# Expert weights moved in 2 MB transfers of neighbouring matrix rows, with token columns and activations regrouped to match

## The chip, the core and the metric

The kernel runs on one core of a Trainium2 chip. The metric is the device time of one execution in microseconds (us), from the start of the program to its end; smaller is better. TensorE (PE in the profile) multiplies matrices, VectorE (DVE), ScalarE (ACT) and GpSimd (POOL) work on elements, and SyncE (SP) issues most of the transfers (DMAs) from the memory of the chip into the core's own. That memory has 128 partitions, and TensorE sums over partitions.

## The reference

A first block of two layers (feed-forward, token mixing, feed-forward) and a second block of one layer (attention, then a mixture of experts) on 256 tokens of 1024 numbers, all in float32. The change touches the last stage:

```python
def moe_ffn(h, w_router, b_router, w_gate_up, b_gate_up, w_down, b_down):
    logits = (h @ w_router).astype(jnp.float32) + b_router.astype(jnp.float32)
    top_val, top_idx = lax.top_k(logits, TOP_K)
    gates = jax.nn.softmax(top_val, axis=-1)
...
    def expert_block(args):
        xe, e = args
        gu = xe @ w_gate_up[e] + b_gate_up[e]
        g = jnp.minimum(gu[:, :D_FF_2], SWIGLU_LIMIT)
        u = jnp.clip(gu[:, D_FF_2:], -SWIGLU_LIMIT, SWIGLU_LIMIT)
        act = (u + 1.0) * (g * jax.nn.sigmoid(SWIGLU_ALPHA * g))
        return act @ w_down[e] + b_down[e]
...
    return jax.ops.segment_sum(y, tok_sorted, num_segments=n)
```

`TOP_K` is 4. An expert's weights are 1024 by 2048 numbers or 8 MB (`w_gate_up`) and 1024 by 1024 or 4 MB (`w_down`); the 32 experts have 384 MB, of the 638 MB that the whole program moves.

## The kernel before

The program runs through its stages once: the first block until about 1130 us, attention until about 1315, routing, and the experts from 1340 to the end. A scheduler puts each engine's instructions into a fixed order ahead of time; buffers come from pools, and a transfer into a buffer waits until the last reader of what was in it is done.

In the first block and attention (the dense part), `piece` (L145) and `natural_parts` (L361) load 1 MB of weights at a time into one of four `raw` buffers. `split` makes two float32r parts of each half: the upper on ScalarE (L177, `wh`, or `dh` for the rows of a feed-forward's second matrix), the rest on VectorE (L178). The last of these four operations frees the buffer.

For the experts, `moe_order` lists the weights in the order of use, 1 MB at a time: of `w_gate_up` eight pieces of 128 rows (a partition receives one row, 8 KB), of `w_down` four pieces of 256 rows (a partition receives two rows that lie 128 rows apart, 4 KB each). `moe_slots` names nineteen 1 MB places, used round and round: two of `rawE`, two halves of `xp`, six slots that attention had, four `raw`, four `raw2`, one `raw3`. `prefetch` issues the next transfer (L1159). Some are issued during attention and routing as places come free, the others as the experts use theirs.

An expert takes 64 places for tokens. For four experts at a time, `tokens` (L1188) selects their tokens of `h2` with matmuls against a 0/1 matrix; its stationary operand is 128 neighbouring columns of `h2`. `gate_up` multiplies (L1209) and adds the bias (L1213). A matmul here has 64 rows of output, and two of them, for the two halves of the columns, stand in different halves of the array. `down` for the expert before transposes the activations (L1227, 128 neighbouring columns each), multiplies (L1235), adds the bias (L1238), scales (L1240, VectorE), turns the gates (L1243, L1245), and adds the result to the tokens (L1249). `leave` (L1261 to L1264) copies the sums and sends them out. `overflow` repeats it for experts with over 64 tokens.

Of the kernel before, what the change touches and what calls it, by code (L numbers as in the profile page):

```python
# [16 lines left out]
P = 128  # L17
# [20 lines left out]
class Kernel:  # L38
    def __init__(self, ctx, tc, a, out):
# [4 lines left out]
        self.raw = pool("raw", 4)  # L44
# [8 lines left out]
        self.uid = 0  # L53
# [13 lines left out]
    # ---------------------------------------------------------------- constants  # L67
# [87 lines left out]
    def conv_block(self, w, h, l):  # L155
        """w = x @ weights, transposed."""
# [7 lines left out]
    def up_block_t(self, w, ab, h, l, t):  # L164
        """As up_block, for 128 tokens."""
# [5 lines left out]
    def split(self, v, low=None, pools=None):  # L171
        """v [P, k, f], 1024 numbers on a partition, as two float32r parts whose sum is v."""
# [16 lines left out]
    # ---------------------------------------------------------------- layer norm  # L189
# [9 lines left out]
    def rstd_wide(self, pool, var, eps, scale):  # L199
        """As rstd: by exponential and logarithm, then a step of Newton's."""  # L200
# [11 lines left out]
    def to_T(self, src, t, ks=range(KD), psum=None, halves=None):  # L212
        """Columns of src, 128 at a time, transposed into self.xT, or into halves, as two float32r parts."""
# [15 lines left out]
    def residual(self, acc, t, scale):  # L229
        """Adds the scaled residual to sums that matmuls have started."""  # L230
# [4 lines left out]
    def add_norm(self, pool, t, acc, eps, g, b, y):  # L235
        """xn[t] = layer norm of acc."""
# [22 lines left out]
    def up_ahead(self, w1, w3, small=False, low=None):  # L259
        """The first pieces, and their parts, one after another."""  # L260
# [92 lines left out]
    # ---------------------------------------------------------------- token mixing  # L353
    def natural_parts(self, srcs, n, q, low=None):
        """The parts of 512 rows of the columns that srcs name."""
        r = self.raw.tile([P, 2048], F32, tag="raw", name=self.n("raw"))
# [9 lines left out]
    def natural(self, srcs, n, parts=None):  # L366
        """[tokens, n] of x @ w for the columns that srcs name, as [P, 2, 512] of PSUM; with parts the first tokens first."""
# [1299 lines left out]
```

## Time and profile before

| | |
|---|---|
| three runs | 2287.51, 2284.88, 2289.31 us; median 2287.51 |
| span of the profiled execution (first to last instruction) | 2285.8 us |
| median less span | 1.7 us |
| TensorE busy | 2177.6 us, 95% of the span |
| first block, attention, routing | about 1340 us |
| experts | about 946 us |
| moved | 637.68 MB, 237193 packets |

The profile gives no time of its own for the profiled execution beyond the span. The time in which an engine is busy is an average over stages; the stages differ, so the rows further down are taken stage by stage. In the trace a float32 matmul leaves two records, so "x8" of L1235 are four matmuls. The trace leaves out no stage, but a few of TensorE's records can be missing.

### The profile page before, as it was taken

To read this page: it belongs to the slowest core of one execution; us is meant where nothing else is said; L and a number is where in the kernel's file an instruction comes from. 1 tells how busy PE (TensorE), PEld (TensorE's weight loads), DVE (VectorE), ACT (ScalarE), POOL (GpSimd) and SP (SyncE) were. 2 spreads that over 40 slices of the span, in tenths; PEclk is the share of its full clock that TensorE was granted. 3 is DMA by queue.
4 is the path that set the end of the run, shared out by engine and by line. 5 is a ranking of instruction groups with operands and counts; after the bars stand their busy time and mean duration, and the time that the engine had idled before them with its cause. 6 is when DMAs were issued, how large, how long until landed. Compare 5 with 4: busy or idle time off the path is not lost. (4 is left out here: it accounts for less than half of the span.)

```text
span 2285.8 us, 28097 instructions
## 1 busy us (share of the span) xinstructions
PE 2177.6 (95%) x11342; PEld 1366.5 (60%) x11343; DVE 1057.9 (46%) x1656; ACT 753.9 (33%) x1110; POOL 191.9 (8%) x216
## 2 busy tenths in 40 slices
PE   7999999999899999999989789999999999999998
PEld 6888877888788887788867553333333333333332
DVE  5866875966776687686676721111111111111111
ACT  4554842555355484255547410000000000000000
POOL 1001222001100122200020300000000000000000
PEclk8999998999999999899999779999999999999999
DMA  9855432956775443275654479999999999999997
GB/s 271 298 184 156 151 119 74 330 187 214 246 256 184 153 150 119 76 248 191 206 190 132 175 299 418 416 417 417 417 416 417 417 418 417 417 417 416 417 417 295
DMA packets 237193, 637.68 MB, mean 279 GB/s; under 512 B 27201, under 2 KB 134689, under 8 KB 204289
## 3 DMA queue, kind: packets, MB, share of 16 engines
q1 hardware_dynamic: 219664, 622.96, 72.0%
q0 software_dynamic: 4048, 11.28, 1.6%
q10 hardware_dynamic: 13344, 1.57, 0.5%
q8 instruction: 91, 1.49, 0.3%
q14 instruction: 46, 0.37, 0.0%
HBM read 633.91 MB, written 1.86 MB: 278 GB/s over the span
## 5 line engine op out<-in xcount | busy, mean ns | idle before, releaser
L178 DVE TENSOR_TENSOR wl<-raw,wh 128x1024 fp32r<-128x1024 f32 x332 | 407.9, 1234 | 190.5 <-ACT wh L177 189.0
L177 ACT ACTIVATE wh<-raw 128x1024 fp32r<-128x1024 f32 (+1 forms) x350 | 366.5, 1051 | 367.6 <-PE w L152 142.8
L1209 PE MATMUL w<-rawm,XT 128*64 128x512 f32 x2048 | 479.5, 597 | 3.0 <-ACT wh L1245 2.1
L152 PE MATMUL w<-xT,wh 128*128 128x512 f32 x1344 | 476.5, 396 | 5.1 <-DVE ab L288 5.1
L153 PE MATMUL w<-xT,wl 128*128 128x256 f32 x1344 | 378.8, 282 | 0.0
L1209 PEld LDWEIGHTS w<-rawm,XT 128*64 128x64 f32 x2048 | 145.5, 137 | 302.0 <-issue 289.2
L1216 DVE TENSOR_SCALAR wl<-w 128x512 f32<-128x512 f32 x32 | 22.1, 692 | 594.3 <-PE w L1213 594.3
L152 PEld LDWEIGHTS w<-xT,wh 128*128 128x128 f32 x1344 | 254.0, 189 | 65.5 <-DVE ab L288 5.8
L153 PEld LDWEIGHTS w<-xT,wl 128*128 128x128 f32 x1344 | 253.4, 189 | 1.6
L1235 PE MATMUL w<-rawm,wh 128*64 128x512 f32 x1024 | 237.3, 600 | 5.7 <-ACT wh L1229 3.7
L300 PE MATMUL m<-wh,gT 128*128 128x512 f32 x592 | 190.9, 393 | 0.0
L1229 ACT ACTIVATE wh<-w 128x512 f32<-128x512 f32 x32 | 19.1, 597 | 449.6 <-PE w L1227 443.0
L1235 PEld LDWEIGHTS w<-rawm,wh 128*64 128x64 f32 x1024 | 67.0, 136 | 145.3 <-issue 130.7
L300 PEld LDWEIGHTS m<-wh,gT 128*128 128x128 f32 x592 | 111.2, 188 | 26.8 <-issue 1.7
L1240 DVE TENSOR_TENSOR wl<-w,wl 128x512 f32<-128x512 f32 x32 | 22.1, 692 | 211.6 <-PE w L1238 211.6
L300 PE MATMUL m<-wl,gT 128*128 128x512 f32 x296 | 116.3, 393 | 0.0
L1218 ACT ACTIVATE wl<-wl 128x512 f32<-128x512 f32 x32 | 20.1, 629 | 236.5 <-DVE wl L1216 236.5
L1197 POOL TENSOR_TENSOR G<-wl 128x256 f32<-128x256 f32 x32 | 22.9, 744 | 834.3 <-PE w L1243 818.3
L377 PE MATMUL w<-wh,xT 128*128 128x512 f32 (+1 forms) x224 | 87.2, 389 | 5.3 <-DVE xT L227 5.3
L375 PE MATMUL w<-wh,xT 128*128 128x512 f32 (+1 forms) x224 | 89.2, 400 | 2.4 <-ACT pre L702 1.9
L376 PE MATMUL w<-wl,xT 128*128 128x512 f32 (+1 forms) x224 | 87.1, 389 | 4.4 <-DVE wl L178 4.4
L1188 PE MATMUL w<-wl,wh 128*128 128x256 f32 (+2 forms) x288 | 69.5, 390 | 4.6 <-ACT wh L1245 4.0
(469 smaller groups left out, 2720.3 us busy)
## 6 DMA issues: line engine op xcount, KB each, us to landing
rawm<-in_w_gate_up_dram SPq DMA_DIRECT2D x252, 1024.0 KB
raw<-in_ffn_w_dram SPq DMA_DIRECT2D x130, 1024.0 KB
rawm<-in_w_down_dram SPq DMA_DIRECT2D x128, 1024.0 KB
raw<-in_w_in_dram SPq DMA_DIRECT2D x36, 1024.0 KB
adaw<-in_w_ada_dram SPq DMA_DIRECT2D x48, 512.0 KB
raw<-in_w_out_dram SPq DMA_DIRECT2D x12, 1024.0 KB
rawm<-in_w_gate_up_dram POOLq DMA_DIRECT2D x4, 1024.0 KB, 7.1
raw<-in_w_in_dram SPq DMA_DIRECT2D x4, 544.0 KB
```

Source lines behind the costliest of these rows:

```text
L152: nc.tensor.matmul(w[:, ab], h[:, k], self.xT[:, k], start=(k == 0), stop=False)
L153: nc.tensor.matmul(w[:, ab, :T], l[:, k], self.xT[:, k, :T], start=False, stop=(k == KD - 1))
L177: nc.scalar.activation(h, v, AF.Copy)
L178: (low or nc.vector).tensor_tensor(l, v, h.bitcast(F32), op=OP.subtract)
L300: mm = lambda g, w, start, stop: nc.tensor.matmul(acc[t][q], g, w[:, 0, q * 512 : (q + 1) * 512], start=start, stop=stop, skip_group_check ...
L375: self.nc.tensor.matmul(w[:, t, :n], xh, h, start=(k == 0), stop=False)
L376: self.nc.tensor.matmul(w[:, t, :n], xh, l, start=False, stop=False)
L377: self.nc.tensor.matmul(w[:, t, :n], xl, h, start=False, stop=(k == KD - 1))
L1188: nc.tensor.matmul(wv[:, k], self.h2[t][:, ks], at[:, t, lo:hi], start=(t == 0), stop=(t == 1))
L1197: self.nc.gpsimd.tensor_tensor(g[:, :n, d], oh[:, t, :n], gate[t][:, :, None].to_broadcast([P, n, 64]), op=OP.mult)
L1209: nc.tensor.matmul(gu[c * 64 : c * 64 + 64, b], XT[:, k], r[:, 0, f0 : f0 + 512], start=(k == 0), stop=False)
L1235: nc.tensor.matmul(td[c * 64 : c * 64 + 64, 1], aT[:, k % 4, k // 4], r[:, j, c * 512 : (c + 1) * 512], start=(k == 0), stop=False)
```

## The change

The experts' weights come in 2 MB transfers. Piece i of `w_gate_up` is 256 rows, of which partition p receives rows 2p and 2p+1: 16 KB that lie together. Piece q of `w_down` is 512 rows, of which partition p receives rows 4p to 4p+3, again 16 KB together. Since TensorE sums over partitions, the other operand has to be grouped alike: `tokens` takes every second column of `h2` (8 bytes apart) as stationary operand, and `down` transposes every fourth column of the activations (16 bytes apart).

There are nine places of 2 MB, so 18 MB ahead where there were 19 MB: `rawE`, `xp`, three of attention, two `raw`, two `raw2`; `raw3` is gone. `raw` is two buffers of 2 MB in the dense part too, where `raw_half` hands out one half and then the other. A buffer is free when both halves are. Bias, scaling and sums are as before. Comments are dropped, so line numbers shift.

```diff
-        self.raw = pool("raw", 4)
+        self.raw = pool("raw", 2)
...
+    def raw_half(self):
+        if self.spare is None:
+            x = self.raw.tile([P, 2, 2048], F32, tag="raw", name=self.n("raw"))
+            self.spare = x[:, 1]
+            return x[:, 0]
+        x, self.spare = self.spare, None
+        return x
+
     def piece(self, src):
-        r = self.raw.tile([P, 2048], F32, tag="raw", name=self.n("raw"))
+        r = self.raw_half()
...
-            self.prefetch(2)
+            self.prefetch(1)
...
-            self.prefetch(4, nc.gpsimd)
+            self.prefetch(2, nc.gpsimd)
...
-        halves = [self.raw2.tile([P, 4, 2 * T], F32R, tag="raw2", name=self.n("xT3")) for _ in range(2)]
-        self.prefetch(10)
+        x3 = self.raw2.tile([P, KD, 2 * T], F32R, tag="raw2", name=self.n("xT3"))
+        halves = [x3[:, 0:4], x3[:, 4:8]]
+        self.prefetch(5)
...
-                yield from (gu[e][k * P : (k + 1) * P, :].rearrange("(o p) f -> p o f", p=P) for k in range(KD))
+                yield from (self.gu_piece(e, i) for i in range(4))
             if e:
-                yield from (dn[e - 1][q * 256 : (q + 1) * 256, :].rearrange("(k p) f -> p k f", p=P) for q in range(4))
+                yield from (self.dn_piece(e - 1, q) for q in range(2))
+
+    def gu_piece(self, e, i):
+        x = self.a["w_gate_up_2"][0]
+        if isinstance(e, int):
+            return x[e][i * 256 : (i + 1) * 256, :].rearrange("(p j) f -> p j f", j=2)
+        return x[bass.ds(e, 1), i * 256 : (i + 1) * 256, :].rearrange("o (p j) f -> p (o j) f", j=2)
+
+    def dn_piece(self, e, q):
+        x = self.a["w_down_2"][0]
+        if isinstance(e, int):
+            return x[e][q * 512 : (q + 1) * 512, :].rearrange("(p s) f -> p s f", s=4)
...
-                ks = slice((k0 + k) * P, (k0 + k + 1) * P)
+                i, j = divmod(k0 + k, 2)
                 for t in range(2):
-                    nc.tensor.matmul(wv[:, k], self.h2[t][:, ks], at[:, t, lo:hi], start=(t == 0), stop=(t == 1))
+                    h = self.h2[t].rearrange("p (i m j) -> p i j m", i=4, j=2)[:, i, j]
+                    nc.tensor.matmul(wv[:, k], h, at[:, t, lo:hi], start=(t == 0), stop=(t == 1))
...
+        av = act.rearrange("p (m s) -> p s m", s=4)
         for s in range(4):
-            nc.tensor.transpose(td[:, 0, s * P : (s + 1) * P], act[:, s * P : (s + 1) * P], self.ident)
+            nc.tensor.transpose(td[:, 0, s * P : (s + 1) * P], av[:, s], self.ident)
...
-        self.raw3 = ctx.enter_context(tc.tile_pool(name="raw3", bufs=1, reuse_waits="tile"))
-        self.prefetch(3)
+        self.prefetch(1)
```

The scheduler puts TensorE's work for an expert into another order. First an expert without token selection, from its gate turn to the next expert's transposes, before. `rawm` is a piece of weights, `XT` the tokens, `m` the sums over experts; a row without "x" is one matmul:

```order
L1243 MATMUL w_13483<-ident,G_13072 128x128
L1235 MATMUL w_13450<-rawm_13462,wh_11589 64x512 x4
L1235 MATMUL w_13450<-rawm_13468,wh_11589 64x512 x4
L1235 MATMUL w_13450<-rawm_13474,wh_11589 64x512 x4
L1238 MATMUL w_13450<-wl_11591,eye_154 64x512 x2
L1209 MATMUL w_13497<-rawm_13498,XT_13372 64x512
L1249 MATMUL m_11863<-wl_11592,wh_11589 128x512
L1249 MATMUL m_11864<-wl_11592,wh_11589 128x512
L1249 MATMUL m_11865<-wl_11592,wh_11589 128x512
L1249 MATMUL m_11866<-wl_11592,wh_11589 128x512
L1209 MATMUL w_13497<-rawm_13498,XT_13372 64x512 x3
```

The same place on TensorE now (L1230 is the gate and up product, L1256 the down product, L1259 its bias, L1270 the sums, L1249 the transposes):

```order
L1264 MATMUL w_13194<-ident,G_12828 128x128
L1256 MATMUL w_13165<-rawm_13181,wh_11477 64x512 x8
L1259 MATMUL w_13165<-wl_11479,eye_154 64x512 x2
L1270 MATMUL m_11744<-wl_11480,wh_11477 128x512
L1270 MATMUL m_11745<-wl_11480,wh_11477 128x512
L1270 MATMUL m_11746<-wl_11480,wh_11477 128x512
L1270 MATMUL m_11747<-wl_11480,wh_11477 128x512
L1230 MATMUL w_13208<-rawm_13209,XT_13094 64x512 x8
L1249 MATMUL w_13258<-ident,wh_11476 128x128 x3
L1230 MATMUL w_13208<-rawm_13219,XT_13094 64x512 x8
L1249 MATMUL w_13258<-ident,wh_11476 128x128
L1230 MATMUL w_13208<-rawm_13229,XT_13094 64x512 x8
```

The single product of the next expert that stood between the bias and the sums is gone from there; the down product's split is 8 and 8 where it was 4 and 12, and the four transposes stand in two places.

In every fourth expert TensorE also selects tokens. The rows after the gate turn, before:

```order
L1188 MATMUL w_13373<-wl_11593,wh_11586 128x256
L1235 MATMUL w_13329<-rawm_13341,wh_11589 64x512 x4
L1188 MATMUL w_13373<-wl_11593,wh_11587 128x256
L1188 MATMUL w_13373<-wl_11593,wh_11586 128x256
L1188 MATMUL w_13373<-wl_11593,wh_11587 128x256
L1235 MATMUL w_13329<-rawm_13347,wh_11589 64x512 x4
L1188 MATMUL w_13373<-wl_11593,wh_11586 128x256
```

And now (L1207 selects tokens):

```order
L1207 MATMUL w_13472<-wl_11481,wh_11474 128x256
L1207 MATMUL w_13472<-wl_11481,wh_11475 128x256
L1207 MATMUL w_13472<-wl_11481,wh_11474 128x256
L1207 MATMUL w_13472<-wl_11481,wh_11475 128x256
L1207 MATMUL w_13472<-wl_11481,wh_11474 128x256
L1256 MATMUL w_13432<-rawm_13448,wh_11477 64x512 x8
```

The same 16 selections stand in three runs where there were five.

In the dense part SyncE's queue holds, at the end of the first feed-forward, before (`raw` buffers each for themselves):

```order
L145 DMA raw_1704<-in_ffn_w_dram 128x8x256
L145 DMA raw_1815<-in_ffn_w_dram 128x2x1024
L145 DMA raw_1837<-in_ffn_w_dram 128x2x1024
L361 DMA raw_1859<-in_w_in_dram 128x4x272
L361 DMA raw_1859<-in_w_in_dram 128x4x16
```

and now:

```order
L154 DMA raw_1688<-in_ffn_w_dram 128x8x256
L154 DMA raw_1688<-in_ffn_w_dram 128x2x1024
L154 DMA raw_1820<-in_ffn_w_dram 128x2x1024
L370 DMA raw_1820<-in_w_in_dram 128x4x272
L370 DMA raw_1820<-in_w_in_dram 128x4x16
```

Neighbouring pieces now share a buffer's name, so the first of a pair waits for both halves of the pair two before.

## Rows read from the trace of the kernel before

**Rows 1.** The page: TensorE's busy time; DMA share (tenths) and GB/s in 40 slices.

```profile
PE 2177.6 (95%) x11342; PEld 1366.5 (60%) x11343; DVE 1057.9 (46%) x1656; ACT 753.9 (33%) x1110; POOL 191.9 (8%) x216
...
DMA  9855432956775443275654479999999999999997
GB/s 271 298 184 156 151 119 74 330 187 214 246 256 184 153 150 119 76 248 191 206 190 132 175 299 418 416 417 417 417 416 417 417 418 417 417 417 416 417 417 295
```

**Rows 2.** Chain that ended last: start us, us, what and number of records.

```profile
1570.86 8.73 PE w L1209 x40
...
1604.14 8.73 PE w L1209 x40
...
1613.89 1.87 PE w L1235 x8
...
1621.43 1.00 PE w L1238 x4
1622.43 1.00 PE w L1209 x2
...
1631.23 8.73 PE w L1209 x40
...
1687.33 2.72 PE w L1209 x11
```

**Rows 3.** Windows: stretch, length, each engine's busy us, PEclk, DMA share, GB/s.

```profile
1360.00:1370.00 10.00, 10.00 (x51) 4.26 (x51) 0.76 (x2) 0.81 (x1) 0.00 (x0) 1.00 0.94 346
...
2200.00:2250.00 50.00, 48.21 (x214) 14.61 (x210) 4.06 (x6) 2.21 (x4) 0.00 (x0) 1.00 1.02 417
...
2270.00:2272.00 2.00, 2.00 (x10) 0.56 (x6) 0.00 (x0) 0.00 (x0) 0.00 (x0) 1.00 0.05 20
```

**Rows 4.** Waits, 2220 to 2286 us, TensorE: total us, times, longest.

```profile
PE w L1235 <- DMA rawm<-in_w_down_dram: 2.0, 3, 0.9
...
PE w L1209 <- DMA rawm<-in_w_gate_up_dram: 0.9, 2, 0.6
```

**Rows 5.** Waits of SyncE's queue, 1400 to 2286 us.

```profile
SPq L1159 <- DMA rawm<-in_w_gate_up_dram: 212.2, 133, 3.4
```

**Rows 6.** Timeline of SyncE's queue: single issues (start us, us, engine, line, transfer).

```profile
1828.87 0.33 SPq L1159 DMA_DIRECT2D rawm<-in_w_gate_up_dram  x1
...
1836.51 0.33 SPq L1159 DMA_DIRECT2D rawm<-in_w_gate_up_dram  x1
...
1848.94 4.30 SPq L1159 DMA_DIRECT2D rawm<-in_w_gate_up_dram  x1
```

**Rows 7.** Timeline of the end, TensorE.

```profile
2274.57 1.07 PE L1238 MATMUL w<-wl,eye 32*64 32x512 f32 x4
...
2276.59 1.99 PE L1249 MATMUL m<-wl,wh 64*128 64x512 f32 x8 [0.94 <-DVE wl L1240]
```

**Rows 8.** Groups, 1340 to 2286 us, loads of stationary operands: busy us, mean ns.

```profile
L1209 PEld LDWEIGHTS w<-rawm,XT 128*64 128x64 f32 x2048 | 145.5, 137 | 302.0 <-issue 289.2 <-DMA rawm<-in_w_gate_up_dram 7.8 <-ACT wh L1245 3.0
...
L1188 PEld LDWEIGHTS w<-wl,wh 128*128 128x128 f32 x257 | 45.4, 190 | 30.5 <-issue 20.7 <-ACT wh L1245 5.7
...
L1227 PEld LDWEIGHTS w<-ident,wh 128*128 128x128 f32 x128 | 13.6, 140 | 30.8 <-issue 30.8
```

**Rows 9.** Timeline, first feed-forward: two `raw` issues and their first splits.

```profile
131.46 8.93 SPq L145 DMA_DIRECT2D raw<-in_ffn_w_dram  x2
...
148.76 1.06 ACT L177 ACTIVATE wh<-raw 128x1024 fp32r<-128x1024 f32 x1 [1.21 <-PE w L152]
```

**Rows 10.** Timeline, end of the first feed-forward: the last `raw` of it.

```profile
182.12 0.37 SPq L145 DMA_DIRECT2D raw<-in_ffn_w_dram  x1
...
187.82 1.05 ACT L177 ACTIVATE dh<-raw 128x1024 fp32r<-128x1024 f32 x1
...
191.29 1.22 DVE L178 TENSOR_TENSOR wl<-raw,wh 128x1024 fp32r<-128x1024 f32 x1
...
203.25 0.50 PE L300 MATMUL m<-dh,gT 128*128 128x512 f32 x1
```

More of the change, by code (lines that the diff above doesn't have):

```diff
@@ L52, in __init__ @@
             setattr(self, name, pool(name, 4, reuse_waits="tile"))
-        self.uid = 0
+        self.uid, self.spare = 0, None
         self.beside = lambda: None
@@ L354, in natural_parts @@
     def natural_parts(self, srcs, n, q, low=None):
-        r = self.raw.tile([P, 2048], F32, tag="raw", name=self.n("raw"))
+        r = self.raw_half()
         v = r[:, : 4 * n].rearrange("p (k f) -> p k f", k=4)
@@ L805, in second_consts @@
         di, mi = (self.biasB[:, i].bitcast(I32) for i in range(2))
[L806 removed]
+        tmp = self.raw_half()
         d, cnt, mf, neg, ln = (tmp[:, i * 384 : (i + 1) * 384] for i in range(5))
@@ L867, in attention @@
             gt, lq, dg = self.att_par
-            s0, s1 = self.slot(), self.slot()
-            xT2 = {4: self.slot([P, 4, 2 * T], F32R)}
-            s2, s3 = self.slot(), self.slot()
-            xT2[0] = self.slot([P, 4, 2 * T], F32R)
+            s01, s23, x2 = self.slot(), self.slot(), self.slot([P, KD, 2 * T], F32R)
+            (s0, s1), (s2, s3) = ([x[:, i * 2048 : (i + 1) * 2048] for i in range(2)] for x in (s01, s23))
+            xT2 = {0: x2[:, 0:4], 4: x2[:, 4:8]}
             xk = lambda k: xT2[k // 4 * 4][:, k % 4]
@@ L1131, in moe_order, with slot @@
     def moe_order(self):
[L1133 removed]
         for e in range(33):
             if e < 32:
[L1136 removed]
+                yield from (self.gu_piece(e, i) for i in range(4))
             if e:
[L1138 to L1140 removed]
+                yield from (self.dn_piece(e - 1, q) for q in range(2))
[8 more added lines that the diff above has]
+            return x[e][q * 512 : (q + 1) * 512, :].rearrange("(p s) f -> p s f", s=4)
+        return x[bass.ds(e, 1), q * 512 : (q + 1) * 512, :].rearrange("o (p s) f -> p (o s) f", s=4)
+    def slot(self, shape=(P, 4096), dtype=F32):
         return self.slotp.tile(list(shape), dtype, tag="slot", name=self.n("slot"))
     def moe_slots(self):
[L1145 removed]
+        self.spare = None
         while True:
[L1147 to L1153 removed]
+            for name in ("rawE", "xp", "slotp", "raw", "slotp", "raw", "raw2", "slotp", "raw2"):
+                tag = {"xp": "xT", "slotp": "slot"}.get(name, name)
+                yield getattr(self, name).tile([P, 4096], F32, tag=tag, name=self.n("rawm"))
     def prefetch(self, n, queue=None):
@@ L1163, in moe_piece @@
         if src is not None:
-            r = self.raw.tile([P, 2048], F32, tag="raw", name=self.n("rawm"))
+            r = self.raw.tile([P, 4096], F32, tag="raw", name=self.n("rawm"))
             v = r.rearrange("p (k f) -> p k f", k=src.shape[1])
@@ L1203, in gate_up @@
         gu = self.wide()
-        for k in range(KD):
-            r = self.moe_piece(src(k))
-            for b in range(2):
-                for c in range(2):
-                    f0 = b * 1024 + c * 512
-                    nc.tensor.matmul(gu[c * 64 : c * 64 + 64, b], XT[:, k], r[:, 0, f0 : f0 + 512], start=(k == 0), stop=False)
+        for i in range(4):
+            r = self.moe_piece(src(i))
+            for j in range(2):
+                k = 2 * i + j
+                for b in range(2):
+                    for c in range(2):
+                        f0 = b * 1024 + c * 512
+                        nc.tensor.matmul(gu[c * 64 : c * 64 + 64, b], XT[:, k], r[:, j, f0 : f0 + 512], start=(k == 0), stop=False)
         for b in range(2):
@@ L1225, in down @@
         td = self.wide()
+        av = act.rearrange("p (m s) -> p s m", s=4)
         for s in range(4):
-            nc.tensor.transpose(td[:, 0, s * P : (s + 1) * P], act[:, s * P : (s + 1) * P], self.ident)
+            nc.tensor.transpose(td[:, 0, s * P : (s + 1) * P], av[:, s], self.ident)
         aT = self.aT
         nc.scalar.activation(aT, td[:, 0].rearrange("p (s c i) -> p s c i", s=4, c=2), AF.Copy)
-        for q in range(4):
+        for q in range(2):
             r = self.moe_piece(src(q))
-            for j in range(2):
-                k = 2 * q + j
+            for s in range(4):
                 for c in range(2):
-                    nc.tensor.matmul(td[c * 64 : c * 64 + 64, 1], aT[:, k % 4, k // 4], r[:, j, c * 512 : (c + 1) * 512],
-                                     start=(k == 0), stop=False)
+                    nc.tensor.matmul(td[c * 64 : c * 64 + 64, 1], aT[:, s, q], r[:, s, c * 512 : (c + 1) * 512],
+                                     start=(q == 0 and s == 0), stop=False)
         for c in range(2):
@@ L1373, in run @@
         self.early.close()
-        self.rawE = ctx.enter_context(tc.tile_pool(name="rawE", bufs=2, side="right", reuse_waits="tile"))
+        self.rawE = ctx.enter_context(tc.tile_pool(name="rawE", bufs=1, side="right", reuse_waits="tile"))
         rb = self.dense.enter_context(tc.tile_pool(name="rowp", bufs=1, side="right", reuse_waits="tile"))
```

19 lines of the change are left out of this document (4 added, 15 removed).

## The prediction

> **What bounds the kernel now.** I read the page first. TensorE is busy for 95% of the span, and from the 25th of 40 slices on the DMA row is full at 416 to 418 GB/s [rows 1]. So the two compete in the experts' stage, and the other 1340 us have slack on the DMA side: no slice there is above 330 GB/s.
>
> The chain that ended last tells which of them sets the end. Through the experts it is TensorE alone: an expert takes 1631.23 - 1604.14 = 27.09 us, and four with one selection of tokens 1687.33 - 1570.86 = 116.47, or 29.12 us an expert [rows 2]. The transfers of one expert, 12 of 1 MB at 417 GB/s [rows 3], take 12 x 2.515 = 30.2 us. The transfers are the slower of the two, by 1.1 us an expert, and live on what was fetched ahead. This is used up just before the end: TensorE's first waits for weights come after 2220, and they are 2.0 + 0.9 us [rows 4]. The last bytes land about 2270 [rows 3]. What is left is TensorE's tail and the way out.
>
> So the end is balanced. Infinitely fast transfers give back no more than about 3 us, while each us by which the transfers get later costs about one. This asymmetry decides the case.
>
> **The transfers.** SyncE's queue waits for landings, eight transfers back in the program's order [rows 5]. So the spacing of its issues is the landing time of earlier pieces. Between 1828.87 and 1836.51 three `w_down` pieces landed (4 KB packets): 2.547 us each. Between 1836.51 and 1848.94 five `w_gate_up` pieces landed (8 KB packets): 2.486 each [rows 6]. Twice the packet saves 0.061 us per MB. No row has 16 KB packets. If the cost goes by the number of packets, 16 KB saves half as much again: 2.456. The two ends are that longer packets gain no more over 8 KB (2.486), and that nothing changes at all (the mix of today, (8 x 2.486 + 4 x 2.547) / 12 = 2.506). I take 2.456, by the trend of the two rows.
>
> The transfers run without a break from about 1370 to 2270, 900 us. 2.456 instead of 2.506 is 2.0%, or 18 us earlier. Against it: 1 MB less lies ready at the start (2.5 us later), and places come free in twos of MB, so that the queue, which already ran short of places once before 1370 (share 0.94) [rows 3], starts its full run some 2 us later. Net: the last bytes land about 13 us earlier, near 2257. At 2.486 it is 2270 - 7 + 4.5, so 2 to 3 us earlier, and TensorE still waits for next to nothing. So the whole 3.0 us of waits go: **-3.0**.
>
> [...]
>
> **TensorE's order.** Two matmuls for the two column halves run at the same time: four take 1.87 and one alone 1.00 [rows 2], so a pair is 0.86 and each run of them has 0.15 on top. Before, a steady expert has one product (x2 records) put between the bias L1238 and the sums L1249; it splits a pair, so an expert pays 25 pair slots instead of 24. Now the slot is saved (-0.86), but the sums wait for VectorE's scaling with nothing between. That is to be seen once before, at the end: L1238 starts at 2274.57, L1249 at 2276.59 [rows 7], 2.02 us where the steady bias took 1.00: +1.02. The split of the transposes costs another run: +0.15. Net +0.3 an expert. In the expert that selects tokens six runs disappear (two of L1235, one of L1209, one of L1227, two of L1188), 6 x 0.15 to 0.2, so -1.0. A group of four: 3 x 0.3 - 1.0, about -0.1; over six or seven such groups **-0.5**, from -2 to +2. The order of the tail has the same length by the same numbers.
>
> **Strided stationary operands.** No stationary operand of the trace is read at a stride, so I bound it. Below: nothing. A load of 128 columns takes 190 ns in L1188, of 64 columns 137 in L1209 [rows 8], so what depends on the columns is about 53 ns for 64, or 106 for 128; reading at half speed adds 106. In `tokens` a record takes about half a 256-column matmul, 0.22 us, and 190 + 106 exceeds this by 0.08, times 257 records: 20 us. In `down` the load of 140 ns hardly shows a part that goes by columns, at most 106, times 128: 14 us. A gain is excluded, since the same columns are loaded. So 0 to 34 us. I take **0**: a load of 128 columns in L1227 costs just 3 ns more than one of 64 in L1209 [rows 8], so reading seems not to be what the load waits for.
>
> **The dense part.** The first piece of a pair now waits for the release three pieces back, and not four. In the steady feed-forward two neighbouring pieces are issued from 131.46 on, the second at the end of a stretch of 8.93 us; the first of them is split at 148.76 [rows 9]. An even piece that goes with its neighbour is issued up to 8.6 us later, still 8.7 us ahead of its split. The smallest lead that is seen to be enough is 187.82 - 182.12 = 5.7 us [rows 10]. So it is hidden there, by the depth of the buffers. The place with least cover is the end of each feed-forward: the last piece moves from 182.12 to the end of L178 at 191.29 + 1.22 = 192.51, lands 5.7 later at 198.2, is split by about 200.5, and is first needed at 203.25 [rows 10]. It fits with 2 to 3 us to spare. Where attention borrows one half for constants the pairs shift once, and I expect a wait of one or two us there. The scheduler also puts the splits of the feed-forwards into another order. **+1.5**, from -2 to +5.
>
> **Sum.** -3.0 - 0.5 + 0 + 1.5 = -2.0. The profiled span of 2285.8 becomes 2283.8, and with the 1.7 us between span and median 2285.5.
>
> **The rivals.**
>
> First, the transfers do not get faster. Then the lesser reserve and the coarser places show: +4.5 us at the last byte, and after it 3.6 us of matmuls (two runs of 1.87, rows 2) where there were 1.87. The waits stay. 2287.5 + 6 = 2293.5, slower. It decides from a rate of about 2.50 us per MB on; below, TensorE is ahead. For it: 417 GB/s look like a ceiling, the same in fifteen slices [rows 1]. Against it: the two rates in rows 6 differ by packet size alone.
>
> Second, the strided reads cost. Half of the bound is +17: 2302, slower. For it: 190 ns against a 0.22 us record leaves little cover. Against it: the 3 ns above. [...]
>
> Third, the pairs of `raw` make the dense part wait: two or three us at each of the feed-forwards' ends and at attention's start, for the reason above with a later landing. +6 in all: 2291.5, slower.
>
> Fourth, TensorE gains more: longer runs also remove waits that the order caused at the beginning of runs, and the dense part's new order happens to fit better. Another -4: 2281.5, faster.
>
> That the change doesn't do what it says isn't likely: 2 MB transfers with 16 KB rows are what the program issues.
>
> **Chances.** The forecast 0.50, the first rival 0.13, the second 0.13, the third 0.10, the fourth 0.14. A measurement can tell about 0.2%, 4.6 us, from no change: under 2282.9 is faster, over 2292.1 slower. The forecast's own range is 2281 to 2290, so a sixth of it (0.08) is faster; with the fourth rival 0.22. The first two rivals are slower, and 0.05 of the third: 0.31. The same: 0.47. The range for 8 in 10 reaches from 2280 over the first and third rivals to the lower half of the second: 2280 to 2297.
>
> **What would show it.** In the changed kernel SyncE's queue should issue 2 MB every 4.91 us, the GB/s row should read 425 or so, and the last bytes should land near 2257; above 4.98 us the first rival is right. TensorE should have no wait for `rawm` after 2220, a steady expert should take 27.4 us, and one with tokens 34.2; where the mean load in the transposes or the selection of tokens is above 0.2 us, the second is. The routing's end and the start of the first expert (about 1340 before) tell about the dense part: over 3 us later speaks for the third. I am wrong altogether if the first block moves by more than the experts do.

## The result, and the profile after

The changed kernel takes 2302.09 us (median of 4 runs, 2299.38 to 2306.62) against 2287.36 for the kernel before in the same comparison: 1.0070 times the time, 95% interval 1.0052 to 1.0088. It is slower by 14.7 us, and outside the range that was forecast. The profiled execution took 2300.92 us, with a span of 2299.1.

The page of the changed kernel answers to [rows 1]. The first line is TensorE's busy time, then the granted clock, the DMA share and the GB/s in 40 slices, then the packets:

```profile
PE 2167.1 (94%) x11342; PEld 1375.1 (60%) x11343; DVE 1063.3 (46%) x1656; ACT 752.8 (33%) x1110; POOL 187.9 (8%) x214
...
PEclk9999999999999999999999879999999999999999
DMA  8854432956775443266554379999999999999994
GB/s 255 311 184 155 142 105 86 326 188 200 266 256 183 151 138 116 73 218 217 177 210 153 123 295 420 412 425 425 427 427 428 428 427 427 428 428 428 427 427 182
DMA packets 193156, 637.63 MB, mean 277 GB/s; under 512 B 24128, under 2 KB 131616, under 8 KB 168448
```

The experts' transfers now run at 427 GB/s and not 417, as the change wants it. TensorE is busy for 10 us less, and the time is still longer. Windows of the end (engines' busy us, clock, DMA share, GB/s) are to be laid beside [rows 3]:

```profile
2200.00:2250.00 50.00, 48.23 (x224) 15.34 (x225) 6.73 (x10) 3.22 (x6) 0.00 (x0) 1.00 1.00 426
2260.00:2270.00 10.00, 10.00 (x52) 3.13 (x50) 2.52 (x4) 0.63 (x1) 0.00 (x0) 1.00 0.36 151
2270.00:2280.00 10.00, 8.67 (x40) 2.89 (x38) 0.85 (x2) 0.98 (x2) 0.00 (x0) 1.00 0.00 0
```

In windows of 2 us the last bytes move between 2266 and 2268 (25 GB/s), before between 2270 and 2272 (20 GB/s). Counted from the first expert's first product (1352.57 and 1340.26), the transfers are done some 16 us earlier.

TensorE's waits from 2220 on, beside [rows 4], hold no transfer any more, only short waits for VectorE's scaling, which the new order makes, and one for ScalarE:

```profile
PE m L1270 <- DVE wl L1261: 3.5, 4, 0.9
PE w L1249 <- ACT wh L1266: 0.5, 1, 0.5
```

So the transfers and the waits for them did what was expected. Where the 14.7 us come from shows when one takes the start of the same TensorE instruction in both traces:

| place | before | after | later by |
|---|---|---|---|
| first feed-forward | 100.02 | 98.66 | -1.36 |
| first mixing, transpose of the convolution's result | 286.61 | 285.25 | -1.35 |
| first mixing, product of gqe and gqd | 309.75 | 312.50 | +2.75 |
| second feed-forward | 419.94 | 421.12 | +1.18 |
| second layer, ahead of mixing's solve | 830.09 | 832.25 | +2.15 |
| second mixing, after the same place | 881.95 | 887.30 | +5.34 |
| last feed-forward, third run of products | 977.90 | 984.46 | +6.56 |
| last feed-forward, 7 us on | 984.58 | 993.80 | +9.21 |
| last feed-forward, 16 us further | 1000.10 | 1011.82 | +11.72 |
| routing | 1332.22 | 1344.54 | +12.31 |
| first expert's first product | 1340.26 | 1352.57 | +12.31 |
| last bias, L1238 | 2274.57 | 2287.35 | +12.78 |

Three steps in the dense part, two at the same place of the two mixings and one at the start of the last feed-forward, make up nearly all of it (4.1, 3.2 and 5.2 us). The experts take 1 us more than before, where 3.5 less were forecast.

One execution has its own chance in such a table. The kernel before and the kernel of "Longer packets without pairs" below give TensorE the same instructions in the same order, and yet the second is 0.5 us ahead at the second place of the table, 3.7 at the fourth and 2.6 at the first expert. So a difference of 3 us between two places says little by itself; the 12.3 us and the steps are read together with the waits that stand at them, and with the kernels below that show them again.

### The profile page after: what moved, and what is told of

Read it like the earlier page. It is cut to its first block, busy times and chain, and to the rows that moved or that the text cites. A ratio compares the mean times of both kernels' runs of the same rounds, so it can differ in the third digit from the quotient of the medians.

```text
span 2299.1 us, 27689 instructions
## 1 busy us (share of the span) xinstructions
PE 2167.1 (94%) x11342; PEld 1375.1 (60%) x11343; DVE 1063.3 (46%) x1656; ACT 752.8 (33%) x1110; POOL 187.9 (8%) x214
## 5 line engine op out<-in xcount | busy, mean ns | idle before, releaser
L1230 PE MATMUL w<-rawm,XT 128*64 128x512 f32 x2048 | 463.3, 599 | 2.1 <-ACT wh L1266 2.1
L1230 PEld LDWEIGHTS w<-rawm,XT 128*64 128x64 f32 x2048 | 141.4, 137 | 279.0 <-issue 270.4
L1256 PE MATMUL w<-rawm,wh 128*64 128x512 f32 x1024 | 232.7, 598 | 3.7 <-ACT wh L1251 3.7
L1256 PEld LDWEIGHTS w<-rawm,wh 128*64 128x64 f32 x1024 | 68.2, 136 | 144.4 <-issue 139.7
L1270 PE MATMUL m<-wl,wh 64*128 64x512 f32 x256 | 63.6, 613 | 18.6 <-DVE wl L1261 18.6
```

Of the source, the lines that this page charges most:

```text
L1230: nc.tensor.matmul(gu[c * 64 : c * 64 + 64, b], XT[:, k], r[:, j, f0 : f0 + 512], start=(k == 0), stop=False)
L1256: nc.tensor.matmul(td[c * 64 : c * 64 + 64, 1], aT[:, s, q], r[:, s, c * 512 : (c + 1) * 512], start=(q == 0 and s == 0), stop=False)
L1270: nc.tensor.matmul(acc[t][c], GT[r, t * P : (t + 1) * P], y[r, :], start=first, stop=first or last, skip_group_check=True)
```

## The three steps in the trace

The first step. SyncE's timeline in the changed kernel (start us, us, engine, line, transfer): a pair of `raw` becomes free, and the last piece of `w_in` and the first of `w_out` are issued 0.4 us apart. Before, the first of them went out about 8 us ahead of the second.

```profile
284.30 0.37 SPq L370 DMA_DIRECT2D raw<-in_w_in_dram  x1
284.71 0.51 SPq L154 DMA_DIRECT2D raw<-in_w_out_dram  x1
```

ScalarE's queue there sends a small matrix `QT` through DRAM, two writes of 128 KB and four reads, to have it in another layout. The reads wait for the writes to land. First the kernel before, then the changed one:

```profile
289.09 0.34 ACTq L1507 DMA_DIRECT2D s<-QT  x1
289.46 0.69 ACTq L1507 DMA_DIRECT2D s<-QT  x1
291.11 0.38 ACTq L1509 DMA_DIRECT2D QTc<-s  x1
```

```profile
287.73 0.34 ACTq L1527 DMA_DIRECT2D s<-QT  x1
...
292.27 2.43 ACTq L1529 DMA_DIRECT2D QTc<-s  x4
294.81 0.38 ACT L626 ACTIVATE gqk<-m 128x256 f32<-128x256 f32 x1 [4.79 <-issue]
295.09 0.25 ACT L627 ACTIVATE cgT<-m 32x128 f32<-32x128 f32 x1
```

From the first write's issue to the first read's it was 2.0 us and is 4.5 us. `cgT`, which has nothing to do with `QT`, stands behind the reads in ScalarE's order: ScalarE is idle for 4.79 us, the last of the reads is issued by 294.70, `cgT` starts at 295.09, and TensorE waits for `cgT` (L630). The waits of TensorE from 284 to 312, before and after:

```profile
PE m L621 <- ACT cgT L618: 0.2, 1, 0.2
```

```profile
PE m L630 <- ACT cgT L627: 1.8, 1, 1.8
```

The wait costs more than its 1.8 us. The windows of the changed kernel show the granted clock (third number from the end): 1.00 until the wait, 0.62 and 0.69 in the ten us behind it, where the kernel before has 1.00 throughout.

```profile
290.00:295.00 5.00, 3.63 (x17) 2.61 (x15) 2.02 (x3) 0.21 (x2) 2.30 (x5) 1.00 0.69 180
295.00:300.00 5.00, 4.61 (x12) 3.45 (x13) 4.80 (x6) 4.37 (x9) 0.00 (x0) 0.62 0.27 27
300.00:305.00 5.00, 5.00 (x17) 3.87 (x17) 1.35 (x2) 3.14 (x5) 0.00 (x0) 0.69 0.60 193
```

So -1.35 becomes +2.75: a step of 4.1 us of which under two are the wait. Up to here TensorE has the same order in both kernels, so the step isn't the order's.

The second mixing repeats it with 1.7 us of wait and a step of 3.2. What the clock adds can be told here, because two kernels of the experiments ("The third step, first try" and "Long transfers or long packets") have the same order on TensorE: they wait 1.8 and 1.6 us at this place, but their clock stays at 1.00, and their steps are 0.8 and 1.9. The same window in the changed kernel and in the first of the two:

```profile
870.00:880.00 10.00, 9.25 (x39) 7.40 (x39) 6.69 (x8) 8.73 (x14) 0.00 (x0) 0.83 0.40 83
```

```profile
870.00:880.00 10.00, 8.24 (x36) 6.12 (x35) 6.22 (x7) 6.59 (x11) 0.95 (x2) 1.00 0.34 52
```

So at this place waits of 1.8 and 1.6 us went with steps of 0.8 and 1.9 at a clock of 1.00, and one of 1.7 with a step of 3.2 at 0.83. At the first place the clock fell in all three (0.81 from 290 to 300 in the changed kernel, 0.83 and 0.89 in the other two).

The third step. At the start of the last feed-forward ScalarE and VectorE need `wr`, 128 KB of router weights that GpSimd's queue loads behind two rows of 512 KB. In the changed kernel the issue-to-landing of `wr` is 13.7 us, before it was 9.7 (transfers by line, the last number is the median):

```profile
wr<-in_w_router_dram POOLq DMA_DIRECT2D x1, 128.0 KB, 9.7
```

```profile
wr<-in_w_router_dram POOLq DMA_DIRECT2D x1, 128.0 KB, 13.7
```

The timeline of the changed kernel shows who stands behind it: ScalarE's copy of `wr`, behind that `tmp`, then VectorE's `ab`, then TensorE.

```profile
992.12 0.42 ACT L868 ACTIVATE wrs<-wr 128x256 fp32r<-128x256 f32 x1 [6.18 <-DMA wr<-in_w_router_dram]
992.44 0.58 ACT L295 ACTIVATE tmp<-w 128x512 f32<-128x512 f32 x1
993.05 0.69 DVE L297 TENSOR_TENSOR ab<-w,tmp 128x512 f32<-128x512 f32 x1
...
993.80 0.79 PE L161 MATMUL w<-xT,wh 128*128 128x512 f32 x1 [3.59 <-DVE ab L297]
```

Before, the same TensorE wait was 0.94 us. The clock is 0.76 from 990 to 995 and 0.56 from 995 to 1000.

## Experiments

**One part alone, and that part undone.** The first kernel is the one before with `raw` in pairs and nothing else.

```diff
-        self.raw = pool("raw", 4)
+        self.raw = pool("raw", 2)
...
-        r = self.raw.tile([P, 2048], F32, tag="raw", name=self.n("raw"))
+        r = self.raw_half()
```

> The kernel before with one part of the change: the four raw buffers are two of 2 MB, handed out in halves, in the dense part and for the experts; the experts' transfers stay at 1 MB, packets and operands as before. The traces put the loss ahead of the experts: the first expert starts 12.3 us later in the changed kernel (1352.57 against 1340.26), and the experts themselves take about as long. Theory (pairs of raw): the dense part gets the whole loss, so the first expert starts near 1352 and the time is 2287.4 + 12 to 14 = 2299 to 2302 us. Rival (the 2 MB transfers for the experts that begin during attention, or the experts' own order): the first expert starts at 1340 as before and the time stays within 3 us of 2287.

Measured: 2306.76 us, 1.0089 times before (1.0072 to 1.0106). The first expert starts at 1360.43, the wait for `cgT` is 2.3 us. The pairs alone cost 20.6 us, 4.8 us over what was expected, and by their median more than the whole change; the two intervals overlap, so that they cost more alone isn't shown. In its profile the second feed-forward is 4.5 us further behind than in the changed kernel's, and 2.9 of this arise after the product of gqe and gqd. In that stretch the mean granted clock from 365 to 395 us is 0.72 here and 0.94 in the changed kernel. The two kernels named above, with the changed kernel's own order on TensorE, have 0.72 too, so this part is the chance of one execution.

The second is the changed kernel with `raw` as four buffers of 1 MB; the experts' pieces that go there are two transfers of 1 MB.

```diff
-        self.raw = pool("raw", 2)
+        self.raw = pool("raw", 4)
...
+                if name == "raw":
+                    yield [self.raw.tile([P, 2048], F32, tag="raw", name=self.n("rawm")) for _ in range(2)]
```

> The changed kernel with that one part undone: raw is four buffers of 1 MB again, everywhere; where the experts' ring comes to raw, a 2 MB piece goes as two transfers of 1 MB with 8 KB packets, all else of the experts as in the changed kernel. Theory (pairs of raw): the first expert starts at 1340 and the experts take what they take in the changed kernel (946.5 us from the first expert's product to the end, less 1 to 2 us because TensorE's clock is not low at their start), so 2285 to 2287 us. Rival (the experts' order and the strided operands cost, and the pairs only hide it): 2295 or more.

Measured: 2286.18 us, 1.0004 (0.9992 to 1.0016) times before. `w_in` and `w_out` go out apart again:

```profile
276.27 0.37 SPq L365 DMA_DIRECT2D raw<-in_w_in_dram  x1
284.34 15.20 SPq L149 DMA_DIRECT2D raw<-in_w_out_dram  x3
```

Its profile has the first expert at 1334; the profiled execution took 2282.24 us, 4 us under the median. So the pairs are the loss, and the rest of the change is worth nothing that can be measured.

**The third step, first try.**

```diff
-        nc.scalar.activation(w[:, :, 0], wr, AF.Copy)
+        nc.gpsimd.tensor_copy(w[:, :, 0], wr)
```

> The changed kernel; the upper part of the router's weights is copied by GpSimd and not by ScalarE, so that ScalarE's queue no longer stands behind the landing of wr at 992 us (6.2 us of idle time before that instruction in the changed kernel, 2.5 before). No other engine's order differs. Theory (a small transfer lands late behind two 1 MB ones, ScalarE waits for it in order, TensorE waits 3.6 us for ScalarE and gets its low clock for some us after): 5 us of the loss go, 2296 to 2298 us; TensorE's wait at the start of that feed-forward falls from 3.6 to about 1 us. Rival (the order of the splits on ScalarE and VectorE is what is late there): the wait stays, 2302.

Measured: 2303.33 us, 1.0081 (1.0064 to 1.0098). Missed. TensorE's wait is 3.5 us as before the edit; ScalarE was free, and VectorE took its place:

```profile
990.21 1.23 DVE L794 SCALAR_TENSOR_TENSOR row<-row,sq 128x1024 f32<-128x1024 f32 x1 [2.49 <-DMA row<-mods]
993.36 0.43 DVE L869 TENSOR_TENSOR wrs<-wr,wrs 128x256 fp32r<-128x256 f32 x1 [1.93 <-POOL wrs L868]
993.71 0.68 DVE L297 TENSOR_TENSOR ab<-w,tmp 128x512 f32<-128x512 f32 x1
```

The edit took away one reader of a late transfer and left the other. It does not speak against the landing as the cause, nor for it. The next kernel for this step changes the landing.

**Long transfers or long packets.** The changed kernel with 2 MB transfers, but rows 128 apart as before.

```diff
-            return x[e][i * 256 : (i + 1) * 256, :].rearrange("(p j) f -> p j f", j=2)
+            return x[e][i * 256 : (i + 1) * 256, :].rearrange("(j p) f -> p j f", j=2)
...
-            return x[e][q * 512 : (q + 1) * 512, :].rearrange("(p s) f -> p s f", s=4)
+            return x[e][q * 512 : (q + 1) * 512, :].rearrange("(s p) f -> p s f", s=4)
```

> The changed kernel with 2 MB transfers, but of rows 128 apart as before: 8 KB packets for the gate and up weights, 4 KB for the down weights, and no strided operands; the order on TensorE, ScalarE and VectorE is that of the changed kernel. Theory 1 (packet size sets the rate): 417 GB/s as in the kernel before instead of 427, transfers end some 20 us later than in the changed kernel, TensorE waits for weights at the end for 4 to 8 us. Theory 2 (the size of a transfer sets it): 427 GB/s, no such waits. Both: a group of four transposes takes about 0.15 to 0.3 us less for an expert than in the changed kernel (its load takes 140 ns and not 207), 5 to 9 us in all; so theory 1 about 2298 to 2304 us, theory 2 about 2293 to 2297.

Measured: 2308.26 us, 1.0093 (1.0074 to 1.0112); 417 GB/s from 1800 to 1850, and TensorE's waits at the experts are back:

```profile
PE w L1255 <- DMA rawm<-in_w_down_dram: 5.0, 7, 1.0
...
PE w L1229 <- DMA rawm<-in_w_gate_up_dram: 3.2, 4, 0.9
```

With 2 MB transfers of 4 and 8 KB packets the rate is the 417 GB/s of the kernel before, and with 16 KB packets it is 427; so here the packet set the rate, not the size of the transfer. The time is 4 us over what the first theory gave; in its profile the dense part ends 5 us later than in the changed kernel's. It also gives the price of the strided operands. The chain of the changed kernel has 0.68 us for four transposes in one run, and of this one 0.59; where they stand in two places it is 0.88 against 0.74. The loads of their stationary operands and of the token columns (busy us, mean ns) are, in the changed kernel,

```profile
L1207 PEld LDWEIGHTS w<-wl,wh 128*128 128x128 f32 x288 | 54.5, 211 | 20.7 <-issue 11.0 <-ACT wh L1266 5.4 <-DVE wl L1193 0.8
...
L1249 PEld LDWEIGHTS w<-ident,wh 128*128 128x128 f32 x128 | 19.4, 207 | 41.3 <-issue 40.6 <-ACT wh L1266 0.8
```

and here

```profile
L1206 PEld LDWEIGHTS w<-wl,wh 128*128 128x128 f32 x288 | 53.0, 205 | 21.9 <-issue 11.0 <-ACT wh L1265 5.4 <-DVE wl L1193 0.7
...
L1248 PEld LDWEIGHTS w<-ident,wh 128*128 128x128 f32 x128 | 14.0, 140 | 41.3 <-issue 40.6 <-ACT wh L1265 0.8
```

From one selection of tokens to the next (four experts) it is 1804.56 - 1687.76 = 116.80 us in the changed kernel and 1807.65 - 1691.39 = 116.26 here. So the strides cost 0.54 a group, some 4 us in all, and the new order by itself saves 0.2 a group against the 116.47 of [rows 2]. The selection's own stretches in the chain are as long with strides as without (2.43, 1.07 and 4.09 against 2.43, 1.06 and 4.08), so the cost is the transposes'.

**Breaking one pair.** The changed kernel, with the open half dropped ahead of mixing's output product, so that `w_out` starts a buffer of its own.

```diff
             def out(ks):
+                self.spare = None
                 acc.extend(self.wide() for _ in range(2))
```

> The changed kernel; at the start of each mixing's output product the open half of a raw buffer is dropped, so that the first piece of w_out starts a buffer of its own and is no longer issued together with the last piece of w_in (284.30 and 284.71 us in the changed kernel, just ahead of ScalarE's round trip of QT through DRAM at 287.7). Later pairs shift by one. Theory (two transfers of 1 MB at once make the small round trip land late, ScalarE stands behind it in order, TensorE waits 1.8 us for cgT and has its low clock after that): the wait for cgT falls to 0.3 us as before, TensorE's clock stays at 1.00 there, and the steps of 4.1 us at 285 to 305 and 3.2 us at 860 to 880 go, together 5 to 7 us: 2295 to 2297. Rival (the new order of the splits makes the steps): the wait stays near 2 us, time 2300 to 2303.

Measured: 2289.88 us, 1.0023 (1.0014 to 1.0032). One line takes back most of the 14.7 us: it leaves 5.0 against the kernel before beside it, and is 12.2 under the changed kernel's median. The first piece of `w_out` is no longer at 285, the reads of `QT` follow the writes after 2.0 us,

```profile
288.75 0.34 ACTq L1528 DMA_DIRECT2D s<-QT  x1
...
290.74 3.16 ACTq L1530 DMA_DIRECT2D QTc<-s  x4
294.00 0.39 ACT L627 ACTIVATE gqk<-m 128x256 f32<-128x256 f32 x1 [2.96 <-PE w L386]
```

the wait for `cgT` is gone, and the clock stays at 1.00. The orders on TensorE, ScalarE and VectorE are the changed kernel's up to 330 us, so at this place the rival (the order of the splits makes the steps) is out. It is more than the expected 5 to 7 us, because the pairs behind it have shifted too: the wait at the last feed-forward is 2.1 us and not 3.6, and the clock at 1.00 there as well.

**The third step, second try.** The changed kernel with `wr` ahead of the two rows on GpSimd's queue.

```diff
-        rows1 = rows(1, 0)
         h = [rb.tile([P, D], F32, tag=f"h{t}", name=f"h{t}") for t in range(2)]
...
             self.route_loads(rb, bp)
+            rows1 = rows(1, 0)
```

> The changed kernel; the router's weights (wr) are issued on GpSimd's queue ahead of the two 512 KB rows and not behind them. Moving the copy from ScalarE to GpSimd had not helped, since VectorE's next step reads wr as well and stood behind the same landing. Theory (wr lands late because the rows share the transfer engines with the 2 MB issued at 973 and the loads after them): wr lands before 988, TensorE's wait at the start of that feed-forward falls from 3.6 to 1 to 2 us (VectorE still waits for a row), its clock stays high, and 2 to 4 us of the step of 5.1 us at 960 to 1000 go: 2297 to 2300. Rival: the wait stays.

Measured: 2299.28 us, 1.0058 (1.0042 to 1.0074). TensorE's wait falls from 3.6 to 2.4 us (1 to 2 were expected), and this place's step from 5.2 to about 3, with the same order on TensorE. What it still waits for is a row. So the landing is the cause of the wait. In the time nothing is shown: the median is 2.8 us under the changed kernel's, but the intervals overlap, and against the kernel before beside it 14.4 us are lost and not 14.7. Which of the transfers around it makes it late (the pair at 973, or the 512 KB loads that SyncE issues behind it) is not told apart.

**Both.**

> The changed kernel with both: the pair broken at the output product, and wr ahead of the rows. Theory: the gains add, 7 to 11 us, so 2291 to 2295. What is left over 2287 is then the low clock at the start of the experts (1.4 us) and smaller waits. Rival: at most one of the two steps goes, 2296 or more.

Measured: 2289.33 us, 1.0014 (1.0005 to 1.0023), TensorE's wait at the last feed-forward is 0.6 us. The gains don't add in the trace: breaking the pair had left 1.3 us of that step, and here none is left. In the time this kernel and the one with the pair broken can't be told apart.

**Four buffers, 2 MB transfers for the experts, `wr` first.**

> The kernel with four raw buffers of 1 MB and the experts' 2 MB transfers, and wr ahead of the rows. TensorE there waits only 0.8 us at the place in question, so 0 to 1.5 us less than without: 2284.5 to 2286.5 us. A candidate that could be ahead of both kernels; the rival is no measurable difference.

Measured: 2286.81 us, 1.0004 (0.9992 to 1.0015). No difference, as the rival had it. In this profile the wait at the place in question is 1.8 us and not 0.8: `wr` lands 8.2 us after its issue (9.8 without the edit), but the rows behind it 12.1 (8.1).

**ScalarE out of the way.** The changed kernel with pairs, `QT`'s round trip issued by SyncE.

```diff
-            nc.scalar.dma_start(s2[m].rearrange("h (b j) i -> (h b) j i", j=16), QT[:, m])
+            nc.sync.dma_start(s2[m].rearrange("h (b j) i -> (h b) j i", j=16), QT[:, m])
...
-                nc.scalar.dma_start(self.QTc[:, m, t], s2[m, :, t * P : (t + 1) * P, :].rearrange("h p i -> p h i"))
+                nc.sync.dma_start(self.QTc[:, m, t], s2[m, :, t * P : (t + 1) * P, :].rearrange("h p i -> p h i"))
```

> The changed kernel, pairs and all; the round trip of QT through DRAM in the token mixing (two writes, four reads) is issued by SyncE and not by ScalarE, so that ScalarE no longer stands between the write and its landing. SyncE then issues the write ahead of the first piece of w_out. Theory (TensorE's wait for cgT comes from ScalarE's queue standing behind that landing): the wait for cgT falls from 1.8 us to 0.5 or less in both layers and TensorE's clock stays at 1.00 after it, 4 to 7 us of the 14.7 go: 2295 to 2298. Rival (what is late is the data itself, which VectorE waits for in any case): the wait moves to VectorE's E and 0 to 3 us go: 2299 to 2302.

Measured: 2288.44 us, 1.0008 (0.9996 to 1.0020), 13.7 us less than the changed kernel. The edit does two things at once: ScalarE no longer stands between write and read, and SyncE issues the write ahead of the first piece of `w_out`, so that the first read follows it after 2.2 us. `cgT` runs 5 us earlier than in the changed kernel, and TensorE's wait for it is gone:

```profile
289.56 0.43 ACT L626 ACTIVATE gqk<-m 128x256 f32<-128x256 f32 x1
289.82 0.26 ACT L627 ACTIVATE cgT<-m 32x128 f32<-32x128 f32 x1
```

That is twice what was expected. A third thing goes with it: the scheduler puts TensorE's products in both mixings into another order, with nine of them moved from ahead of the product of gqe and gqd to behind it. So the place at which TensorE is now 5 us ahead of the kernel before isn't a fair one. Where all kernels have the same work behind them, from the transpose of the convolution's result to the first product of `z` and `E`, the first mixing takes 52.1 us here, 59.1 in the changed kernel and 55.0 before, the second 52.4, 57.5 and 54.6. So 5.2 us are gained on the kernel before too; whether by the earlier landing, by ScalarE's free queue or by the new order is not told apart. Part is lost again at the last feed-forward, where TensorE's wait behind `wr` is 4.4 us.

**Longer packets without pairs.** The kernel before, with neighbouring rows in twos for the down weights only (8 KB packets everywhere).

```diff
-(dn[e - 1][q * 256 : (q + 1) * 256, :].rearrange("(k p) f -> p k f", p=P) for q in range(4))
+(dn[e - 1][q * 256 : (q + 1) * 256, :].rearrange("(p k) f -> p k f", k=2) for q in range(4))
...
+        av = act.rearrange("p (q m j) -> p q j m", q=2, j=2)
-            nc.tensor.transpose(td[:, 0, s * P : (s + 1) * P], act[:, s * P : (s + 1) * P], self.ident)
+            nc.tensor.transpose(td[:, 0, s * P : (s + 1) * P], av[:, s // 2, s % 2], self.ident)
```

> The kernel before with one small edit: a 1 MB piece of the down weights is 256 rows of which a partition receives rows 2p and 2p+1 (8 KB together instead of twice 4 KB); the activations are transposed by every second column, 8 bytes apart, within 256. No order differs on TensorE, ScalarE or VectorE, and raw stays four buffers. By the two rates of the trace of before all pieces then take 2.486 us: 29.8 us an expert, and the transfers end 7 us earlier. Theory: TensorE's 2.9 us of waits at the end go, and transposes at 8 bytes cost nothing (the load of the token columns at 8 bytes took 211 ns against 205 in one row, that of the activations at 16 bytes 207 against 140): 1 to 3 us faster than before, 0.05 to 0.13%. Rival: 8 bytes cost half as much as 16, 0.07 us an expert, 2 us, and nothing is gained.

Measured: 2285.18 us, 1.0000 (0.9988 to 1.0012). 421 GB/s, no waits for weights at the end; but the transposes at 8 bytes load as slowly as those at 16 (207 ns), and four of them take 0.68 us again, 0.09 more for each of 32 experts, 3 us. It gives back what the waits gave.

```profile
L1228 PEld LDWEIGHTS w<-ident,wh 128*128 128x128 f32 x128 | 18.2, 207 | 30.8 <-issue 30.8
```

**The two edits on both kernels.** `QT` by SyncE and `wr` first, on the kernel before:

> The kernel before (four raw buffers, 1 MB transfers) with the two edits that take the small transfers out of the way: QT's round trip issued by SyncE and not by ScalarE, and wr ahead of the rows on GpSimd's queue. In the changed kernel the first of them took TensorE 5 us ahead of the kernel before at the place of the step in the first mixing. Theory (ScalarE's queue stands behind QT's landing in the kernel before too): 3 to 7 us faster than before, 2280 to 2283, ahead of both kernels. Rival (there the landing was early enough, TensorE's wait for cgT is only 0.2 us): no difference.

Measured: 2281.58 us, 0.9979 (0.9969 to 0.9989). It beats both kernels: 4.9 us, 0.21%. The mixings take 52.2 us each, together 5.3 less than before, which is about the whole gain; the order on TensorE is changed here as well. `wr` first gives nothing that this profile shows: TensorE's wait there is 2.8 us and was 0.9. And on the changed kernel:

> The changed kernel, pairs and all, with the same two edits. Theory (the pairs cost only through the small transfers that land late behind them): wr's wait falls from 4.4 to 2 us or less, so 2 to 4 us less than with QT on SyncE alone (2288.4): 2284.5 to 2286.5, the time of the kernel before or a little less. Rival (the pairs also cost elsewhere): 2287 or more.

Measured: 2285.09 us, 0.9994 (0.9982 to 1.0005), with the pairs in place. 17 us less than the changed kernel, by two edits that touch neither pairs nor experts. TensorE's wait at the last feed-forward is 2.0 us. Its median is 3.5 us above that of the kernel before with the same edits, at the edge of what the two intervals can tell.

## Why the prediction was wrong

**What bounds the kernel: right.** TensorE bounds the experts and the transfers had been just late enough to show: the 2.9 us of waits for weights went, and TensorE is as busy from 2200 to 2250 as before (48.2 of 50 us in both).

**The transfers: right in kind, nearly in size.** 2.456 us per MB was taken, 427 GB/s is 2.456. The last bytes were to land 13 us earlier; relative to the first expert they land about 16 us earlier. The waits of 2.9 us went, as the -3.0 says. From the mix of 4 and 8 KB to 8 KB alone to 16 KB the rows of the traces give 417, 421 and 427 GB/s. 427 over 421 is 1.4%, where the trend of the two rows had 1.2% (2.486 over 2.456).

**TensorE's order: right.** -0.1 a group was forecast; without the strides the group measures -0.2.

**Strided operands: the value taken was wrong, the bounds held.** 0 was taken, since a load of 128 columns took 3 ns more than one of 64. That comparison did not show what a strided read costs: the transposes' load went from 140 to 207 ns, and 4 us in all were lost. The token columns cost nothing, as taken. By the sign that the prediction set (a mean load above 0.2 us) the second rival was right in the transposes; for the selection of tokens the sign could say nothing, since its load over that window is 205 ns without strides. Transposes at 8 bytes took the same 207 ns as those at 16. The second rival gave strided reads 17 us, about four times their price. Its time, 2302, is the one that was measured, by luck: the strides made 4 us of the loss, and the dense part the rest.

**The experts' sum.** -3.5 was forecast and +1.0 measured: the waits are gone (-2.9) and the order saves (-0.2 in each of seven or eight groups), but the strides cost 4 and the first expert's product 1.6 more, at the low clock.

**The dense part: the step that failed.** +1.5 was taken, -2 to +5 as bounds, and it was +12.3 at the start of the first expert. The argument was that each piece still lands early enough for its own splits. For TensorE this held where it was looked for: ScalarE waits 42.4 us in all for pieces of the feed-forwards and not 28.5, but no step stands at the end of the first of them. It asked only whether the moved transfers would be in time for themselves. It didn't ask what else travels at the moment to which they were moved: that two pieces now leave together, that a round trip of 256 KB leaves 3 us after them, and that an engine stands in order behind that round trip (ScalarE, idle for 4.79 us). The row that would have told it was in the trace of before: 0.2 us of wait for `cgT` is a wait with no cover at all. The third rival named the pairs, gave them 6 us, and put them at the feed-forwards' ends and attention's start; the places and the mechanism were others. By the prediction's last sign (wrong altogether if the first block moves by more than the experts do) it was wrong altogether: the dense part moved by 12.3 us and the experts by 1.

**A wait's price.** Three waits of 1.7 to 3.6 us made steps of 3 to 5, with TensorE's granted clock down behind each: 0.62 and 0.69 in the two stretches of 5 us after the first, 0.83 over the 10 us around the second, 0.76 and 0.56 from 990 to 1000 at the third. No wait was priced so. The price isn't fixed: at the second place, with the same order, the clock was 0.83 in one kernel and 1.00 in two others.

**Left open.** The first expert's gate and up product starts at the low clock (0.50 from 1350 to 1355, 0.72 from 1355 to 1360) and takes 16.5 us in the changed kernel where it took 15.0 (0.77 from 1340 to 1345). This doesn't go with the change: with the pairs it takes 14.9 (`QT` by SyncE) and 16.6 (`QT` by SyncE and `wr` first), and the kernel before with longer down packets, which has the order of the kernel before on TensorE, has 16.5. What sets it is open. Open too is which transfer makes `wr` and the rows late, and which of its three effects makes the gain of moving `QT` to SyncE.

## What to carry to other kernels

When a transfer is moved or joined with another, look not only at its own readers but at the small transfers that leave in the same few microseconds, and at which engine waits for them in order: here ScalarE's queue issued the write of `QT`, could issue the read only 4.5 us later, and `cgT`, which reads nothing of it, started after that. A wait of TensorE's is not its whole price: 1.8 us of it went with a step of 4.1 us where the granted clock was 0.62 behind it, and with 0.8 where it stayed at 1.00. And a buffer pool that is shared with the stage one tunes belongs to the other stages too: four buffers of 1 MB and two of 2 MB hold the same, and the kernel took 2286.18 us with the first and 2302.09 with the second.

## What was not expected of the hardware

128 KB written to DRAM took 2.0 us from issue to the point where its readers could be issued, with 1 MB under way ahead of it, and 4.5 us with 2 MB; over both mixings of all the kernels in which ScalarE issues it, it is 1.7 to 2.0 us where the two pieces leave apart and 4.5 to 4.9 where they leave together. In the transposes a stationary operand of float32 read at every second column loaded in 207 ns as at every fourth, against 140 ns unstrided; in the selection of tokens, at 211 against 205 ns, the time shows nothing of it.
